# Attention stage of a hybrid encoder layer: query swap placed a tile ahead of use, wider buffer rings, memory weights transposed on TensorE alone

## The chip, the cores and the metric

One core of a Trainium2 chip runs one program. The metric is the device time in microseconds (us) from a run of the whole program; the kernel before has three runs. Its engines are called as the profile calls them: PE (TensorE; PEld its weight loads), DVE (VectorE), ACT (ScalarE), POOL (GpSimd), and SP (SyncE), which here does nothing but issue DMAs. Each engine takes its own instructions strictly in order.

## What is computed

Two sequences (4096 and 1024 tokens, width 1024) go through one layer. A combined projection gives Hyena channels, six attention heads, four memory heads and gates. The part that matters here is the attention:

```python
for window, dil in ((128, 1), (512, 4), (2048, 16)):      # dilated windows
    logits = einsum(q_blocks, k_band) * scale + bias       # masked to |rel| <= R
    p = exp(logits - max); s = sum(p)
    outs.append(einsum(p, v_band) / s); lses.append(m + log(s))
y_att = sum(softmax(lses) * outs)                          # merged over the windows
p = softmax(einsum('blhe,bmhe->bhlm', qm, km) * scale)     # 4 heads, 256 memory tokens
y_mem = einsum('bhlm,bmhe->blhe', p, vm)
out = x + (concat(hyena, y_att, y_mem) * silu(gate)) @ w_out
```

## The kernel before, in words

The program weaves two streams on PE. `dense()` projects queries, keys and values and then, in `gates`, the gates (products into tile `zg`, 1920 matmuls through the helper `mm3`, lines 282 to 284). `side()` does the long convolutions, the memory keys and values, and then `attention`. `weave` gives the next piece to the stream whose sum of nominal costs is lower; the costs are what the generators `yield`, and those of attention are scaled by `K_A` = 0.88 while gates run. PE's order is exactly the order in which this is written. The order on the other engines is chosen when the program is built: a list scheduler places each instruction where its own simulated clock finds it ready, and breaks ties by priority, which is the order of emission.

Attention works on 84 groups of up to 256 query rows: 64 groups of the dilated windows, 8 of which are pairs of 64-row sequences, and 20 memory groups. A group has two tiles of 128 rows (a pair has one), so there are 160 tiles, 120 of windows and 40 of memory.

- `load_group` (lines 923 to 973) loads a group two groups ahead (`AHEAD` = 2): DMA transposes bring `qT` (lines 948, 943, 935 for memory) and `kT` (947, 942), plain DMAs bring `v`. For a window group it ends with two DVE copies that swap the halves of the queries, `qS<-qT` (line 971), in a ring of two buffers. Memory groups have no swap.
- `scores` (lines 1005 to 1058) makes products `s` on PE from `qT` (1048) and `qS` (1051), or from `kmT` for memory (1043). DVE reduces each head at once into `pt` with its row maximum `mx` (line 1055). `s` has three PSUM buffers.
- `exps` (1060 to 1070) negates the maximum on DVE (`nm`, 1065) and takes exponentials on ACT (1067). After two heads (`XT` = 2) it calls `crossbar`, which on POOL splits the two heads into halves `hl` (1083, 1084) and issues one DMA transpose `hx<-hl` (1086) on SP.
- `turns` (1090 to 1105) transposes the other heads on PE, two at a time (`tt`, line 1098, four 128x128 blocks, two PSUM buffers), and ACT and DVE copy them out as `th` and `tl` (1102, 1103), four buffers each.
- `values` (1107 to 1127), four tiles behind the scores (`VLAG`), multiplies `th`, `tl` and `hx` with `v` into `yp`, and `attended` brings it out through `y`, two buffers (POOL line 1156, ACT 1157, or DVE 1150 for memory) and a store on SP.

Within a step the four generators take turns by the string `ORDER = "etevsteeesvvsetesvsetse"` (s scores, e exponentials, t turns, v values). When attention ends, the output stage begins: it loads `w_out` (`wos`), splits it, merges the windows (`y<-yc` to `ya`), and its products `oo` start when the last gate product is done.

Of the kernel before, what the change touches and what calls it, by code (L numbers as in the profile page):

```python
# [12 lines left out]
F32 = mybir.dt.float32  # L13
F32R = mybir.dt.float32r
F16 = mybir.dt.float16
# [7 lines left out]
P = 128  # L23
# [3 lines left out]
H = 6  # L27
# [11 lines left out]
YW = VH + H  # L39
# [108 lines left out]
XT, VLAG = 2, 4  # L148
# [33 lines left out]
class Layer:  # L182
# [745 lines left out]
    def load_group(self, pool, g):  # L928
        i, nc = g["seq"], self.nc
        dil, r = g.get("dil", 1), g.get("r", 0)  # L930
        rows = self.rows[i].rearrange("(n d) c -> d n c", d=dil)
        vr = self.vrows[i].rearrange("(n d) c -> d n c", d=dil)
        qT = g["qT"] = pool.tile([P, 6, 256], F16, tag="qT", name="qT", bufs=AHEAD + 1)
        if "mem" in g:
            nc.sync.dma_start_transpose(out=qT[:, 0:4], in_=self.rows[i][g["q0"]:g["q0"] + 256, C_MQ:C_K])
            return
        kT = pool.tile([P, 6, 384], F16, tag="kT", name="kT", bufs=AHEAD + 1)
        nk = g["k1"] - g["k0"]
        v = pool.tile([P, 3, VW], F16, tag="v", name="v", bufs=2)
        if g["pair"]:  # L940
            for a in range(2):
                nc.sync.dma_start_transpose(out=kT[:, :, 64 * a:64 * a + 64], in_=rows[r + a, :, C_K:ROW])
                nc.sync.dma_start_transpose(out=qT[:, :, 64 * a:64 * a + 64], in_=rows[r + a, :, C_Q:C_MQ])
                self.ld(v[64 * a:64 * a + 64, 0, :], vr[r + a])
            g["chunks"] = {0: 0}
        else:
            nc.sync.dma_start_transpose(out=kT[:, :, :nk], in_=rows[r, g["k0"]:g["k1"], C_K:ROW])
            nc.sync.dma_start_transpose(
                out=qT[:, :, :g["nq"]], in_=rows[r, g["q0"]:g["q0"] + g["nq"], C_Q:C_MQ]
            )  # L950
            cuts = [g["k0"]] + list(range(g["q0"] + 64, g["k1"], 128))
            ends = cuts[1:] + [g["k1"]]
            g["chunks"] = {s: j for j, s in enumerate(cuts)}
            full = [j for j, (s, e) in enumerate(zip(cuts, ends)) if e - s == 128]
            part = [j for j, (s, e) in enumerate(zip(cuts, ends)) if e - s != 128]
            if full:
                f0, nf = full[0], len(full)
                assert full == list(range(f0, f0 + nf))
                self.ld(
                    v[:, f0:f0 + nf, :],  # L960
                    vr[r, cuts[f0]:cuts[f0] + 128 * nf].rearrange("(j p) c -> p j c", p=P),
                )
            for j in part:
                k = ends[j] - cuts[j]
                p0 = P - k if j else 0
                nc.gpsimd.memset(v[P - k:P, j, :] if p0 == 0 else v[0:p0, j, :], 0.0)
                self.ld(v[p0:p0 + k, j, :], vr[r, cuts[j]:ends[j]])
        g["kT"], g["v"] = kT, v
        qS = g["qS"] = pool.tile([P, 6, 256], F16, tag="qS", name="qS", bufs=2)
        for a in range(2):  # L970
            nc.vector.tensor_copy(  # L971
                qS[64 * a:64 * a + 64, :, :g["nq"]], qT[64 - 64 * a:P - 64 * a, :, :g["nq"]]
            )
# [18 lines left out]
    def attention(self, pool, ps):  # L992
        nc = self.nc
        zero = pool.tile([P, 1], F32, name="zero", bufs=1)
        nc.vector.memset(zero, 0.0)
        groups = self.work_list()
# [3 lines left out]
        self.load_tables(pool)  # L1000
        for g in groups[1:AHEAD]:
            self.load_group(pool, g)
        yield IDLE_A
        tiles = [(gi, t) for gi, g in enumerate(groups) for t in range(g["nq"] // P)]
        state = {}

        def scores(n):
            gi, t = tiles[n]
            g = groups[gi]
            if t == 0 and gi + AHEAD < len(groups):  # L1010
                while groups[gi + AHEAD]["seq"] not in self.done:
                    yield 500
                self.load_group(pool, groups[gi + AHEAD])
            mem = "mem" in g
            i, q0 = g["seq"], g["q0"] + t * P
            st = state[n] = dict(g=g, q0=q0, mem=mem, H=HM if mem else H)
            if mem:
                W, ls = NMEM, self.lsc[:, 1, 0:1]
                st["chunks"] = [(0, 0), (P, 1)]
                st["v"], st["lo"] = self.vm[i], HM * E1  # L1020
                units = ((0, 1), (2, 3))
            else:
                ls = self.lsc[:, 0, 0:1]
                if g["pair"]:
                    ks, ke, tb, t0 = 0, 128, self.tabp, 0
                    st["chunks"] = [(0, 0)]
                else:
                    ks, ke = max(0, q0 - 64), min(g["n"], q0 + 192)
                    tb, t0 = self.tab[g["cf"]], ks - (q0 - 64)
                    st["chunks"] = [(0, g["chunks"][ks]), (ke - ks - P, g["chunks"][q0 + 64])]  # L1030
                W, kc = ke - ks, ks - g["k0"]
                st["v"], st["lo"] = g["v"], VH
                units = ((0, 2), (1, 3), (4,), (5,))
            st["W"] = W
            pt = st["pt"] = pool.tile([P, H, 256], F32, tag="pt", name="pt", bufs=3)
            mx = st["mx"] = pool.tile([P, H], F32, tag="mx", name="mx", bufs=4)
            qs = slice(t * P, (t + 1) * P)
            for heads in units:
                s = ps.tile([P, 2, 256], F32, tag="f", name="s", bufs=3)
                for a, h in enumerate(heads):  # L1040
                    if mem:
                        for half in range(2):
                            nc.tensor.matmul(
                                s[:, a, :], g["qT"][:, h, qs], self.kmT[i][:, 4 * half + h, :],
                                start=(half == 0), stop=(half == 1),
                            )
                        continue
                    nc.tensor.matmul(  # L1048
                        s[:, a, :W], g["qT"][:, h, qs], g["kT"][:, h, kc:kc + W], start=True, stop=False,
                    )  # L1050
                    nc.tensor.matmul(  # L1051
                        s[:, a, :W], g["qS"][:, h, qs], g["kT"][:, h, kc:kc + W], start=False, stop=True,
                    )
                for a, h in enumerate(heads):
                    nc.vector.tensor_tensor_reduce(  # L1055
                        out=pt[:, h, :W], in0=s[:, a, :W], in1=zero.to_broadcast([P, NMEM]) if mem else tb[:, h, t0:t0 + W], scale=ls,
                        scalar=-3.0e38, op0=ALU.add, op1=ALU.max, accum_out=mx[:, h:h + 1],
                    )
                yield 215 * len(heads)

        def exps(n):
            st = state[n]
            nh, pt, W = st["H"], st["pt"], st["W"]
            nm = st["nm"] = pool.tile([P, H], F32, tag="nm", name="nm", bufs=VLAG + 1)
            nc.vector.tensor_scalar_mul(nm[:, :nh], st["mx"][:, :nh], -1.0)  # L1065
            for h in range(nh):
                nc.scalar.activation(out=pt[:, h, :W], in_=pt[:, h, :W], func=AF.Exp, bias=nm[:, h:h + 1])  # L1067
                if h + 1 == XT:
                    crossbar(st)
                yield 0  # L1070

# [18 lines left out]
        def turns(n):  # L1090
            st = state[n]
            pt, chunks = st["pt"], st["chunks"]
            st["p"] = []
            for pr in range(XT // 2, st["H"] // 2):
                tt = ps.tile([P, 2, 2, P], F32, tag="e", name="tt", bufs=2)
                for ci, (w0, vj) in enumerate(chunks):
                    for a in range(2):
                        nc.tensor.transpose(tt[:, a, ci, :], pt[:, 2 * pr + a, w0:w0 + P], self.ident)  # L1098
                th = pool.tile([P, 2, 2, P], F16, tag="th", name="th", bufs=4)
                tl = pool.tile([P, 2, 2, P], F16, tag="tl", name="tl", bufs=4)  # L1100
                n = len(chunks)
                nc.scalar.activation(out=th[:, :, :n], in_=tt[:, :, :n], func=AF.Copy)  # L1102
                nc.vector.tensor_tensor(out=tl[:, :, :n], in0=tt[:, :, :n], in1=th[:, :, :n], op=ALU.subtract)  # L1103
# [3 lines left out]
        def values(n):  # L1107
            st = state[n]
            chunks, v, lo = st["chunks"], st["v"], st["lo"]
            last = len(chunks) - 1  # L1110
            yp = ps.tile([P, 512], F32, tag="gf"[n % 2], name="yp", bufs=(1, 3)[n % 2])
            heads = list(range(XT, st["H"])) + list(range(XT))
            st["p"] += [(st["hx"][:, 0, h], st["hx"][:, 1, h]) for h in range(XT)]
            for pr in range(st["H"] // 2):
                for a in range(2):
                    h = heads[2 * pr + a]
# [23 lines left out]
    def attended(self, pool, st, yp):  # L1140

        nc = self.nc
        g, q0 = st["g"], st["q0"]
        y = pool.tile([P, YW], F32, tag="y", name="y", bufs=2)
        if st["mem"]:
            sm = pool.tile([P, HM], F32, tag="sm", name="sm", bufs=3)
            yv = yp[:, :HM * E1].rearrange("p (h e) -> p h e", e=E1)
# [528 lines left out]
```

## Time and profile before

| | |
|---|---|
| median of 3 runs | 3090.1 us (3088.88 to 3095.87) |
| the profiled execution | 3090.2 us, its span 3088.4 us |
| PE busy | 2783.8 us, 90% of the span |
| DVE / ACT / POOL busy | 2087.6 / 1690.0 / 1350.3 us |
| chain that ended last, by engine | PE 27%, DMA 10%, DVE 7% |
| its largest single entry | DMA `qT<-rows`, 6% |

The span runs from the first to the last instruction of the core; the run's own time is 1.8 us longer. PE is busy for most of the span, so the question for a stretch is what it idles for. A wait is named after what ended it. "PEclk" is the mean clock that was granted to PE as a share of full speed; the records know two levels, 1.2 and 2.4 GHz, so 0.5 and 1.0.

### The profile page before, as it was taken

To read this page: it belongs to the slowest core of one execution; us is meant where nothing else is said; L and a number is where in the kernel's file an instruction comes from. 1 tells how busy PE (TensorE), PEld (TensorE's weight loads), DVE (VectorE), ACT (ScalarE), POOL (GpSimd) and SP (SyncE) were. 2 spreads that over 40 slices of the span, in tenths; PEclk is the share of its full clock that TensorE was granted. 3 is DMA by queue.
4 is the path that set the end of the run, shared out by engine and by line. 5 is a ranking of instruction groups with operands and counts; after the bars stand their busy time and mean duration, and the time that the engine had idled before them with its cause. 6 is when DMAs were issued, how large, how long until landed. Compare 5 with 4: busy or idle time off the path is not lost. (4 is left out here: it accounts for less than half of the span.)

```text
span 3088.4 us, 55692 instructions
## 1 busy us (share of the span) xinstructions
PE 2783.8 (90%) x19620; PEld 1724.7 (56%) x19620; DVE 2087.6 (68%) x5374; ACT 1690.0 (55%) x3187; POOL 1350.3 (44%) x1574
## 2 busy tenths in 40 slices
PE   5898888988999887986998989999898899999999
PEld 2343444434544444543456666676666665778887
DVE  8778888778757861452657766776666666766663
ACT  5776666433679873472336666666565564323321
POOL 3246777343236661252324333343243443655551
PEclk9999999999999999998999999999999999999999
DMA  7655444565588867585679999999898989777762
GB/s 195 199 154 161 134 127 136 172 180 185 197 233 226 217 179 200 219 178 114 178 183 250 225 208 212 224 227 189 200 220 194 196 176 305 259 235 252 247 227 97
DMA packets 761954, 610.80 MB, mean 198 GB/s; under 512 B 514814, under 2 KB 702358, under 8 KB 758218
## 3 DMA queue, kind: packets, MB, share of 16 engines
q1 hardware_dynamic: 761674, 607.23, 73.7%
q8 instruction: 155, 2.54, 0.3%
q14 instruction: 125, 1.02, 0.1%
HBM read 289.08 MB, written 200.32 MB: 158 GB/s over the span
## 5 line engine op out<-in xcount | busy, mean ns | idle before, releaser
L1067 ACT ACTIVATE pt<-pt,nm 128x256 f32<-128x256 f32 (+2 forms) x880 | 349.8, 472 | 175.9 <-DVE nm L1065 170.0
L282 PE MATMUL z<-wA,hA 128*128 128x512 f16 (+1 forms) x960 | 352.7, 367 | 34.9 <-DVE vr L476 23.6
L283 PE MATMUL z<-wA,hA 128*128 128x512 f16 (+1 forms) x960 | 352.6, 367 | 0.0
L284 PE MATMUL z<-wA,hA 128*128 128x512 f16 (+1 forms) x960 | 352.3, 367 | 0.0
L1055 DVE CUSTOM_DVE_ANT_0 pt<-s,tab,lsc 128x256 f32<-128x256 f32 (+1 forms) x672 | 277.7, 448 | 83.2 <-PE s L1051 73.5
L282 PE MATMUL zh<-hB,wh 128*128 128x512 f16 x720 | 279.8, 389 | 15.1 <-ACT zb L879 14.8
L283 PE MATMUL zh<-hB,wh 128*128 128x512 f16 x720 | 279.5, 388 | 1.6 <-DVE hB L387 1.6
L284 PE MATMUL zh<-hB,wh 128*128 128x512 f16 x720 | 278.9, 387 | 0.0
L282 PE MATMUL oo<-wo,mhi 128*128 128x512 f32 x640 | 257.2, 402 | 8.2 <-DVE xr L1553 2.5
L284 PE MATMUL oo<-wo,mlo 128*128 128x512 f32 x640 | 253.9, 397 | 0.4 <-POOL mlo L1532 0.4
L283 PE MATMUL oo<-wo,mhi 128*128 128x512 f32 x640 | 253.7, 396 | 0.0
L282 PE MATMUL zg<-hG,wg 128*128 128x512 f16 x640 | 246.8, 386 | 0.0
L283 PE MATMUL zg<-hG,wg 128*128 128x512 f16 x640 | 246.5, 385 | 0.0
L284 PE MATMUL zg<-hG,wg 128*128 128x512 f16 x640 | 246.1, 385 | 0.0
L1083 POOL CAST hl<-pt 128x256 f16<-128x256 f32 (+1 forms) x212 | 104.1, 505 | 320.0 <-ACT pt L1067 242.9
L1103 DVE TENSOR_TENSOR tl<-tt,th 128x512 f16<-128x512 f32 (+1 forms) x280 | 187.5, 672 | 58.5 <-ACT th L1102 56.9
L1102 ACT ACTIVATE th<-tt 128x512 f16<-128x512 f32 (+1 forms) x280 | 160.1, 574 | 117.6 <-PE yp L1124 54.3
L1048 PE MATMUL s<-kT,qT 128*128 128x256 f16 (+2 forms) x720 | 165.1, 260 | 45.0 <-DVE mx L1055 43.3
L1098 PE MATMUL tt<-ident,pt 128*128 128x128 f32 x1088 | 171.9, 280 | 30.0 <-DVE tl L1103 25.4
L1338 ACT ACTIVATE kt<-kp,rn 64x384 f32<-64x384 f32 x328 | 188.0, 573 | 13.6 <-PE kp L1332 8.4
L1084 POOL TENSOR_TENSOR hl<-pt,hl 128x256 f16<-128x256 f32 (+1 forms) x212 | 191.4, 910 | 6.8
L893 DVE SCALAR_TENSOR_TENSOR u<-zb,cw,u 128x512 f32<-128x512 f32 (+2 forms) x180 | 163.4, 910 | 25.0 <-ACT u L889 23.2
(303 smaller groups left out, 7277.9 us busy)
## 6 DMA issues: line engine op xcount, KB each, us to landing
y<-yc SPq DMA_DIRECT2D x120, 198.0 KB
yc<-y SPq DMA_DIRECT2D x112, 198.0 KB
xt<-in_x SPq DMA_DIRECT2D x40, 512.0 KB
hts<-hB SPq DMA_DIRECT2D x10, 2048.0 KB
hA<-hts SPq DMA_DIRECT2D x40, 512.0 KB
rows<-rw SPq DMA_DIRECT2D x40, 512.0 KB
hG<-hts SPq DMA_DIRECT2D x10, 2048.0 KB
gt<-go SPq DMA_DIRECT2D x80, 256.0 KB
```

Source lines behind the costliest of these rows:

```text
L282: nc.tensor.matmul(out, pick_l(lh, k), pick_r(rh, k), start=(k == 0), stop=False)
L283: nc.tensor.matmul(out, pick_l(lh, k), pick_r(rl, k), start=False, stop=False)
L284: nc.tensor.matmul(out, pick_l(ll, k), pick_r(rh, k), start=False, stop=(k == n - 1))
L893: nc.vector.scalar_tensor_tensor(out=u[:, :w], in0=zb[:, c0 + d:c1 + d], scalar=cw[:, j, tap:tap + 1], in1=u[:, :w], op0=ALU.mult, op1=ALU ...
L1048: nc.tensor.matmul(s[:, a, :W], g["qT"][:, h, qs], g["kT"][:, h, kc:kc + W], start=True, stop=False,)
L1055: nc.vector.tensor_tensor_reduce(out=pt[:, h, :W], in0=s[:, a, :W], in1=zero.to_broadcast([P, NMEM]) if mem else tb[:, h, t0:t0 + W], scal ...
L1067: nc.scalar.activation(out=pt[:, h, :W], in_=pt[:, h, :W], func=AF.Exp, bias=nm[:, h:h + 1])
L1084: nc.gpsimd.tensor_tensor(out=hl[:, 1, :, c], in0=src, in1=hl[:, 0, :, c], op=ALU.subtract)
L1098: nc.tensor.transpose(tt[:, a, ci, :], pt[:, 2 * pr + a, w0:w0 + P], self.ident)
L1102: nc.scalar.activation(out=th[:, :, :n], in_=tt[:, :, :n], func=AF.Copy)
L1103: nc.vector.tensor_tensor(out=tl[:, :, :n], in0=tt[:, :, :n], in1=th[:, :, :n], op=ALU.subtract)
L1338: nc.scalar.activation(out=kt[64 * b:64 * b + 64, a], in_=kp[64 * a:64 * a + 64, :DH], func=AF.Identity, scale=rn[64 * a:64 * a + 64, a * ...
```

## The change

The swap leaves `load_group` and becomes a function of its own. It is called for the first group before the loop, and for every later group at the start of the last tile of the group ahead of it. Memory tiles get `xt` = 0 in place of `XT` = 2: no `crossbar`, no `hl` and `hx`, and a second turn on PE for the two heads that went through them. `th` and `tl` have six buffers in place of four, `y` four in place of two.

```diff
         g["kT"], g["v"] = kT, v
+
+    def swap_queries(self, pool, g):
+
+        if "mem" in g:
+            return
+        nc, qT = self.nc, g["qT"]
         qS = g["qS"] = pool.tile([P, 6, 256], F16, tag="qS", name="qS", bufs=2)
         for a in range(2):
             nc.vector.tensor_copy(
...
         for g in groups[1:AHEAD]:
             self.load_group(pool, g)
+        self.swap_queries(pool, groups[0])
         yield IDLE_A
...
                 self.load_group(pool, groups[gi + AHEAD])
+            if (t + 1) * P == g["nq"] and gi + 1 < len(groups):
+                self.swap_queries(pool, groups[gi + 1])
             mem = "mem" in g
...
                 W, ls = NMEM, self.lsc[:, 1, 0:1]
-                st["chunks"] = [(0, 0), (P, 1)]
+                st["chunks"], st["xt"] = [(0, 0), (P, 1)], 0
...
+                st["xt"] = XT
                 W, kc = ke - ks, ks - g["k0"]
...
-                if h + 1 == XT:
+                if h + 1 == st["xt"]:
                     crossbar(st)
...
-            for pr in range(XT // 2, st["H"] // 2):
+            for pr in range(st["xt"] // 2, st["H"] // 2):
...
-                th = pool.tile([P, 2, 2, P], F16, tag="th", name="th", bufs=4)
-                tl = pool.tile([P, 2, 2, P], F16, tag="tl", name="tl", bufs=4)
+                th = pool.tile([P, 2, 2, P], F16, tag="th", name="th", bufs=6)
+                tl = pool.tile([P, 2, 2, P], F16, tag="tl", name="tl", bufs=6)
...
-            heads = list(range(XT, st["H"])) + list(range(XT))
-            st["p"] += [(st["hx"][:, 0, h], st["hx"][:, 1, h]) for h in range(XT)]
+            heads = list(range(st["xt"], st["H"])) + list(range(st["xt"]))
+            st["p"] += [(st["hx"][:, 0, h], st["hx"][:, 1, h]) for h in range(st["xt"])]
...
-        y = pool.tile([P, YW], F32, tag="y", name="y", bufs=2)
+        y = pool.tile([P, YW], F32, tag="y", name="y", bufs=4)
```

The built programs show where the instructions went. First DVE at the swap of one window group in the middle of attention; the rows are in DVE's order, numbers tell buffers apart, and lines of the changed kernel are 10 further down (977 is the swap, 1065 the reduction, 1075 `nm`, 1113 `tl`). Before:

```order
L1055 ISA pt_17844,mx_17845<-s_17897,tab0_15041,lsc_849 128x256
L1055 ISA mx_17845 128x1
L971 COPY qS_17744<-qT_17738 64x1536 x2
L1055 ISA pt_17844,mx_17845<-s_17902,tab0_15041,lsc_849 128x256
L1055 ISA mx_17845 128x1
L1103 TENSOR_TENSOR tl_17915<-tt_17909,th_17914 128x512
L1065 TENSOR_SCALAR nm_17906<-mx_17845 128x6
```

The same group in the changed program:

```order
L1065 ISA pt_17865,mx_17866<-s_17932,tab0_15038,lsc_849 128x256
L1065 ISA mx_17866 128x1
L1065 ISA pt_17865,mx_17866<-s_17940,tab0_15038,lsc_849 128x256
L1065 ISA mx_17866 128x1
L977 COPY qS_18082<-qT_17747 64x1536 x2
L1075 TENSOR_SCALAR nm_17944<-mx_17866 128x6
L1113 TENSOR_TENSOR tl_17953<-tt_17947,th_17952 128x512
```

`pt_17844` and `pt_17865` are the same tile, the last of the group two ahead of the swapped one. The swap went from ahead of that tile's sixth reduction to behind it; it was emitted a whole group later, as its number 18082 tells, and did not move by a group.

Second, SP between one query load and the next that are followed by the two tiles of a memory group. Before:

```order
L948 DMA_TRANSPOSE qT_21138<-rows0_75 128x6x256
L195 DMA v_20694<-vrows1_106 128x774
L195 DMA v_20694<-vrows1_106 64x774 x2
L1086 DMA_TRANSPOSE hx_21021<-hl_21018 128x8x128
L198 DMA yc0_0_83<-y_21097 128x396
L1086 DMA_TRANSPOSE hx_21120<-hl_21117 128x8x128
L198 DMA yc0_1_84<-y_21192 128x396
L195 DMA v_20929<-vrows0_76 128x3x774
L198 DMA gt0_2_89<-go_21305 128x512
L198 DMA yc0_1_84<-y_21292 128x396
L1086 DMA_TRANSPOSE hx_21228<-hl_21223 128x8x128
```

In the changed program:

```order
L948 DMA_TRANSPOSE qT_21198<-rows0_75 128x6x256
L198 DMA gt0_2_89<-go_21162 128x512
L195 DMA v_20767<-vrows1_106 128x774
L195 DMA v_20767<-vrows1_106 64x774 x2
L198 DMA yc0_0_83<-y_21158 128x396
L198 DMA yc0_1_84<-y_21261 128x396
L195 DMA hG_15482<-hts0_4_99 128x8192
L195 DMA v_20999<-vrows0_76 128x3x774
L198 DMA gt0_2_89<-go_21381 128x512
L1096 DMA_TRANSPOSE hx_21294<-hl_21289 128x8x128
```

The two DMA transposes of the memory tiles (`hx_21021`, `hx_21120`) are gone; a 2 MB load of the gates (`hG`) has come forward into the stretch.

## Rows read from the trace of the kernel before

**Rows 1.** Busy time by stretch: stretch, us, PE, PEld, DVE, ACT, POOL, PEclk, DMA share, GB/s

```profile
1588.00:2562.00 974.00, 888.01 (x9878) 633.60 (x9876) 673.92 (x2479) 597.34 (x1370) 364.11 (x606) 0.97 0.97 211
2562.00:2603.50 41.50, 40.63 (x191) 18.60 (x189) 22.69 (x43) 18.72 (x23) 12.84 (x9) 1.00 0.98 351
2603.50:3088.40 484.90, 472.93 (x2115) 381.17 (x2115) 299.98 (x666) 140.51 (x173) 250.74 (x191) 1.00 0.66 224
```

**Rows 2.** Waits of PE, 1588 to 2562 us: total us, times, longest

```profile
PE s L1048 <- DVE mx L1055: 43.3, 32, 5.6
PE tt L1098 <- DVE tl L1103: 25.4, 22, 3.0
PE s L1043 <- DVE mx L1055: 5.9, 3, 4.4
```

**Rows 3.** DVE in order of time, around one swap: start, us, what, idle before

```profile
2178.90 0.42 DVE L1103 TENSOR_TENSOR tl<-tt,th 128x256 f16<-128x256 f32 x1
2184.45 1.12 DVE L971 COPY qS<-qT 64x1536 f16<-64x1536 f16 x2 [5.13 <-DMA qT<-rows]
```

**Rows 4.** PE in order of time, the same moment

```profile
2181.34 0.38 PE L284 MATMUL zg<-hG,wg 128*128 128x512 f16 x1
2186.15 1.01 PE L1043 MATMUL s<-kmT,qT 128*128 128x256 f16 x4 [4.43 <-DVE mx L1055]
...
2187.81 0.63 PE L282 MATMUL zg<-hG,wg 128*128 128x512 f16 x1
```

**Rows 5.** Waits of the other engines, 1588 to 2562 us

```profile
POOL hl L1083 <- ACT pt L1067: 242.9, 98, 7.2
...
POOL y L1156 <- DMA yc<-y: 158.2, 63, 6.2
DVE qS L971 <- DMA qT<-rows: 105.9, 44, 6.2
...
ACT th L1102 <- PE yp L1124: 54.3, 50, 3.8
```

**Rows 6.** SP's issues in order of time, ahead of that swap's query load

```profile
2163.67 3.48 SPq L935 DMA_TRANSPOSE qT<-rows  x1
2167.25 4.64 SPq L1086 DMA_TRANSPOSE hx<-hl  x1
2171.99 0.53 SPq L198 DMA_DIRECT2D ym<-y  x1
2172.61 2.12 SPq L947 DMA_TRANSPOSE kT<-rows  x1
...
2180.53 1.46 SPq L948 DMA_TRANSPOSE qT<-rows  x1
```

**Rows 7.** Instructions on tile hx: SP's issues, ns min/median/max

```profile
L1086 SPq DMA_TRANSPOSE hx<-hl x160: 1206/1271/5327, 1608.2 to 2556.8; - x160
```

**Rows 8.** DMA packets, 1588 to 2562 us

```profile
DMA packets 453444, 205.96 MB, mean 211 GB/s; under 512 B 400590, under 2 KB 441792, under 8 KB 451904
```

**Rows 9.** Chain that ended last, two turns: start, us, what

```profile
1906.67 0.44 PE tt L1098 x4
...
1924.62 0.85 PE tt L1098 x4
```

**Rows 10.** Groups of instructions by form, 1588 to 2562 us: busy us, mean ns

```profile
L1103 DVE TENSOR_TENSOR tl<-tt,th 128x512 f16<-128x512 f32 x264 | 180.9, 687 | 56.7 <-ACT th L1102 55.1
...
L1102 ACT ACTIVATE th<-tt 128x512 f16<-128x512 f32 x264 | 154.1, 586 | 107.6 <-PE tt L1098 45.2 <-PE yp L1124 44.8 <-PE yp L1123 17.1
```

**Rows 11.** ACT in order of time, the last tile of attention

```profile
2561.46 0.50 ACT L1157 ACTIVATE y<-yp 128x390 f32<-128x390 f32 x1 [1.37 <-PE yp L1124]
```

**Rows 12.** DVE in order of time, the first merged tile of the output

```profile
2593.39 0.55 DVE L1504 TENSOR_TENSOR ya<-y 128x384 f32<-128x384 f32 x1
```

**Rows 13.** PE in order of time, the first output product

```profile
2603.53 0.50 PE L282 MATMUL oo<-wo,mhi 128*128 128x512 f32 x1 [0.90 <-ACT mhi L1531]
```

## The prediction

> **What bounds the kernel now.** I read the busy time by stretch first. Attention, woven with gate products, takes the stretch from 1588 to 2562 us [rows 1]: PE is busy for 888 of 974 us there, so 86 us are idle; the change touches nothing before it. The stretch's DMA share is 0.97 and no other engine is busy for more than 70%. The waits of PE say what the idle time is for: 43.3 + 25.4 + 5.9 = 74.6 us until DVE has freed a PSUM buffer, of scores or of a turn [rows 2]. So DVE is late, though it is idle for 300 us. The two timelines show why. DVE ends its work at 2179.3, reaches a swap whose query load has not landed, and stands for 5.13 us [rows 3]; PE runs on until its buffers are full and then stands for 4.43 us [rows 4]. All in all DVE stands 105.9 us, 44 times, in front of a swap [rows 5], 1.65 us for each of the 64 swaps. And the load is late because SP comes late to it: its issues follow each other within 0.1 us, transposes of 3.48, 4.64 and 2.12 us among them, until the load goes out at 2180.5 [rows 6], after DVE had begun to wait. So the chain is SP and the DMA engines, then DVE at the swap, then PE.
>
> **The change, part by part.** The sum is made against the profiled execution's 3090.2 us, 0.1 us above the median of the three runs.
>
> *The swap itself* costs the same copies, 64 pairs in both programs. Its words promise a load two tiles more to land. The built order does not keep that promise: in both programs the swap stands behind the scores of the group two ahead, where its buffer comes free, because the scheduler is at liberty to bring an instruction forward. Over the 64 swaps I count in the order 13.2 reductions (a little over two tiles) between a swap and the first one that needs it before, 13.0 now. The query loads stand where they were on SP too: 8.1 tiles ahead of use by the stores that precede them, in both. So I price this edit at nothing. What it does move is the sixth reduction of the tile, now mostly ahead of the swap, which frees one more score buffer before a wait, and `nm`, now mostly behind it, which holds ACT. I let them cancel.
>
> *Memory tiles.* Forty tiles lose `hx` and gain a turn. On PE a turn of four transposes takes 0.44 us at full clock and 0.85 us at half [rows 9]: 17.6 to 34 us, and with a mean clock of 0.97, that is 6% of the time at half clock, 19 us. All of this is added to PE's queue and none of it is hidden. ACT gets 40 x 0.586 = 23 us and DVE 40 x 0.687 = 27 us [rows 10]; they are covered by the 377 and 300 us that these engines idle in the stretch, and if DVE's cover failed the 27 us would come on top. POOL loses the splitting, worth nothing, since it is busy for 364 us only.
>
> *What the missing `hx` gives back.* SP spends 1.271 us on an issue [rows 7] and rarely pauses, so 40 issues are 51 us of its time, or 0.80 us for each of the 64 intervals between swaps, against a wait of 1.65 us: 48%. The DMA engines gain too. Their 0.97 of 974 us is 945 us for 206 MB. Packets under 512 B are 400590 [rows 8], and a row of a transposed block is 256 B by the code, so 103 MB are transposes and 103 MB plain. The plain stretch behind moves 351 GB/s at a share of 0.98 [rows 1], so the plain bytes take 289 us and the transposes 656 us, 1.6 ns a packet. One `hx` is eight blocks of 128 rows; 40 of them are 40960 packets, 67 us of 945. The Trainium skill (Advanced Engine Details and Errata, X-Bar Transpose) says otherwise: "TRN2 transpose DMAs are as fast as regular DMAs". By that the `hx` would give back less than half of the 67 us, and the sum would near the second rival's; the trace speaks against it, with 211 GB/s at 0.97 beside 351 GB/s at 0.98. Between all of PE's 74.6 us kept and all of it gone I take the 48%: 36 us.
>
> *The clock.* After the wait at 2186 the same gate product stands for 0.63 us in place of 0.38 [rows 4], so PE was then granted the lower of its two levels. With 6% of 974 us at half clock about 29 us of work are lost in the stretch, at most all of it is won back, at least nothing; I take a third, 10 us.
>
> *The buffers.* POOL stands 158.2 us for the store of `y`, and ACT 54.3 us for the values that free `th` [rows 5]; both waits should go. Neither engine holds PE directly. POOL's lateness delays `hx` and thereby SP, but 98 times `hl` waits for ACT and not for POOL [rows 5]. Bounds: nothing, or the 39 us of stalls that the term above leaves. I take 6 us, near the lower end, because the work behind these waits is mostly early. Next in line is ACT's exponential for `nm`.
>
> *The end of attention.* A turn counts 430 in the weave, so attention's stream advances more slowly against gates and takes more of them with it: in PE's order 120 gate products stand behind attention's last value product, 189 before. The 69 are only moved. But they covered something: attention ends at 2562.0 [rows 11], the first merged tile that the output needs is ready at 2593.9 [rows 12], 32.0 us later, and the gates behind lasted until then, so that the first output product waits 0.90 us only [rows 13]. Now they last 120 x 40.63/191 = 25.5 us, and PE stands 6 us. At best loads start earlier and this is nothing; at worst the next tiles come late too, 15 us.
>
> Sum: 3090.2 + 19 - 36 - 10 - 6 + 6 = 3063 us.
>
> **The rivals.** *Nothing is given back.* The loads' place in SP's order, not SP's load, makes them late: SP then waits for PE and POOL instead of for itself, DVE still stands 106 us. Then PE pays for the turns and the join: 3090 + 19 + 6 = 3115 us. For it: the order is the same, and at the end of a stretch SP also waits for buffers. Against it: the closed row of issues in rows 6. It decides if less than a third of the 74.6 us goes.
>
> *Only bytes count.* SP's gaps are then filled by waiting for the DMA engines, and a transposed byte takes no longer than a plain one: 40 x 0.262 MB at 351 GB/s [rows 1] are 30 of 945 us, 3%. Stalls and clock then give back a tenth, 10 us: 3105 us. The Trainium skill (DMA: Bandwidth & Descriptors, Issuing engines are not separate DMA queues) has such a rule: initiating a DMA takes sequencer time that is "usually small relative to the DMA itself". Here an issue holds SP 1.271 us [rows 7], and SP issues back to back [rows 6], which speaks against the rival.
>
> *It cancels.* Stalls and clock give back about 25 us, a third less than I take, and the turns and the join eat it: 3090 us.
>
> *All stalls go.* The backlog on SP is a matter of bursts, and a tenth less load ends it, or the loads do come earlier as the change says: 3090 + 25 - 75 - 29 = 3011 us. Against it speaks that loads of 2 MB for the gates remain, one of which now stands ahead in the row that the order shows.
>
> **How the numbers follow.** My forecast has 0.56, all stalls gone 0.14, cancelled 0.13, nothing given back 0.09, bytes alone 0.08. A measurement of this kernel tells about 0.2%, 6 us, from no change. Faster is the forecast and the third gain, 0.70; the same 0.13; slower 0.17. The range reaches from the fast rival to just short of the slow two, 3010 to 3098 us, which leaves 0.17 out; it covers the bounds of the turns (17.6 to 34), of the join (0 to 15) and of the stalls (a quarter of them to all).
>
> **What would show it.** In the changed profile the wait of DVE for `qT` should be 45 to 70 us, not near zero and not 106; PE's waits for DVE some 40 us; the waits of `y` on POOL and of `th` on values nearly gone; 1248 transposes of `tt`, not 1088; PE idle for some 7 us before the first output product; attention some 25 us shorter. If DVE still stands for 100 us at the swap the explanation by SP's load is wrong; if it stands for none, the swap or the load moved after all.

## The result and the profile after

The changed kernel took 3111.5 us (median of 4 runs, 3107.4 to 3116.6), the kernel before 3089.5 us. The ratio of the two is 1.0064, with a 95% interval from 1.0042 to 1.0087: **slower by 20 us**, where I had forecast 27 us faster. The profiled execution of the changed kernel has a span of 3105.6 us, 17.2 us more than that of before.

I cut both traces at three events on PE: the first score product, attention's last value product, the first output product. In brackets stands the time in which PE idled.

| us (PE idle) | before | changed |
|---|---|---|
| up to the first score product | 1592.6 | 1591.4 |
| to attention's last value product | 968.7 (86.0) | 981.9 (71.0) |
| to the first output product | 42.2 (0.9) | 34.1 (7.3) |
| to PE's end | 480.6 (7.7) | 493.9 (18.2) |

69 gate products more lie ahead of the last value product in the changed kernel; at 40.63/191 us each [rows 1] they are 14.7 us. Without them attention took 967.2 us, 1.5 us less than before. I had forecast 33 us less (19 - 36 - 10 - 6). Behind attention 8.1 of those 14.7 us came back, so 6.6 us were lost, and the output then took 13.3 us longer. So all of the loss lies behind attention, and the gain that should have outweighed it did not come.

The same stretch as in rows 1, then the first 40 us of the output (stretch, us, PE, PEld, DVE, ACT, POOL, PEclk, DMA share, GB/s):

```profile
1588.00:2562.00 974.00, 903.43 (x9927) 648.66 (x9926) 678.80 (x2500) 615.62 (x1398) 288.04 (x518) 0.97 0.89 199
...
2600.00:2640.00 40.00, 24.12 (x97) 19.26 (x98) 31.10 (x62) 13.46 (x17) 26.40 (x20) 0.79 0.94 319
```

The DMA engines have 8% of the stretch to themselves that they had not before (share 0.89 for 0.97), and yet PE's granted clock stands at 0.97 as it did. The waits, 1588 to 2600 us, which answer to rows 2 and 5:

```profile
POOL hl L1093 <- ACT pt L1077: 330.4, 77, 16.2
DVE qS L977 <- DMA qT<-rows: 110.8, 43, 5.8
POOL y L1166 <- DMA yc<-y: 81.8, 35, 7.5
PE s L1058 <- DVE mx L1065: 48.5, 32, 5.0
PE tt L1108 <- DVE tl L1113: 15.5, 11, 4.3
```

DVE waits for its query loads 110.8 us, not 45 to 70; before it was 105.9. PE's waits for DVE add to 64 us, not 40. The wait of `y` was halved and that of `th` on values is gone. SP's issues ahead of a late query load, in order of time, show why fewer issues did not help:

```profile
2141.88 0.54 SPq L198 DMA_DIRECT2D yc<-y  x1
2145.44 1.48 SPq L195 DMA_DIRECT2D v<-vrows  x3
2147.14 0.42 SPq L198 DMA_DIRECT2D gt<-go  x1
2147.66 2.50 SPq L1096 DMA_TRANSPOSE hx<-hl  x1
2150.21 0.58 SPq L198 DMA_DIRECT2D yc<-y  x1
2150.88 1.45 SPq L948 DMA_TRANSPOSE qT<-rows  x1
```

SP ended an issue at 2142.4, issued nothing for 3 us until 2145.44, and then took 2.50 us for an `hx`, about twice the median of rows 7. So SP had time to spare, and the query load behind still went out at 2150.88 only. DVE's swap was ready for it 3.35 us before it could start:

```profile
2155.01 1.12 DVE L977 COPY qS<-qT 64x1536 f16<-64x1536 f16 x2 [3.35 <-DMA qT<-rows]
```

Over 1588 to 2565 us I summed SP's DMA issues, each split into the shortest tenth's time of its kind and what lies above it, and the gaps between them: the shortest times fell from 554.5 to 497.9 us, while gaps and excess rose from 415.1 to 472.4 us. All of the rise is in the gaps, from 178.2 to 248.1 us; the excess inside the issues went from 236.9 to 224.3 us. **What SP no longer issued became gaps between its issues.**

The start of the output, on ACT (attention's last tile), DVE (the first merged tile) and PE:

```profile
2573.31 0.50 ACT L1167 ACTIVATE y<-yp 128x390 f32<-128x390 f32 x1 [0.40 <-PE yp L1134]
```

```profile
2605.85 0.52 DVE L1514 TENSOR_TENSOR ya<-y 128x384 f32<-128x384 f32 x1
```

```profile
2598.79 0.38 PE L284 MATMUL zg<-hG,wg 128*128 128x512 f16 x1
2606.42 1.33 PE L1535 MATMUL ot<-ident,ya 128*128 128x128 f32 x5 [7.25 <-DVE ya L1514]
2607.40 0.78 PE L282 MATMUL oo<-wo,mhi 128*128 128x512 f32 x1
...
2630.11 1.30 PE L1535 MATMUL ot<-ident,ya 128*128 128x128 f32 x5 [9.33 <-DVE mw L1504]
```

The first merged tile is ready 33 us after attention's end, as before [rows 11, 12], but the gates end 7 us earlier than that. PE waits 7.25 us, which I had forecast as 6. I had not forecast the second wait, 9.33 us, 24 us later. The first output product behind the first wait takes 0.78 us and not 0.50 [rows 13], and the granted clock of these 40 us is 0.79.

### The profile page after: what moved, and what is told of

Read it like the earlier page. It is cut to its first block, busy times and chain, and to the rows that moved or that the text cites. A ratio compares the mean times of both kernels' runs of the same rounds, so it can differ in the third digit from the quotient of the medians.

```text
span 3105.6 us, 55808 instructions
## 1 busy us (share of the span) xinstructions
PE 2802.1 (90%) x19780; PEld 1746.0 (56%) x19780; DVE 2094.8 (67%) x5414; ACT 1713.0 (55%) x3227; POOL 1275.3 (41%) x1494
## 5 line engine op out<-in xcount | busy, mean ns | idle before, releaser
L282 PE MATMUL zh<-hB,wh 128*128 128x512 f16 x720 | 279.8, 389 | 15.0 <-ACT zb L879 14.7
L1113 DVE TENSOR_TENSOR tl<-tt,th 128x512 f16<-128x512 f32 (+1 forms) x320 | 214.3, 673 | 64.5 <-ACT th L1112 63.0
L1093 POOL CAST hl<-pt 128x256 f16<-128x256 f32 (+1 forms) x172 | 78.8, 476 | 433.2 <-ACT pt L1077 330.4
L1112 ACT ACTIVATE th<-tt 128x512 f16<-128x512 f32 (+1 forms) x320 | 182.2, 574 | 125.2 <-PE tt L1108 124.2
L1108 PE MATMUL tt<-ident,pt 128*128 128x128 f32 x1248 | 194.8, 278 | 19.2 <-DVE tl L1113 15.5
L1348 ACT ACTIVATE kt<-kp,rn 64x384 f32<-64x384 f32 x328 | 188.0, 573 | 13.2 <-PE kp L1342 8.1
L1108 PEld LDWEIGHTS tt<-ident,pt 128*128 128x128 f32 x1248 | 150.6, 143 | 55.4 <-issue 14.9
```

Source lines behind the costliest of these rows:

```text
L282: nc.tensor.matmul(out, pick_l(lh, k), pick_r(rh, k), start=(k == 0), stop=False)
L1093: nc.gpsimd.tensor_copy(hl[:, 0, :, c], src)
L1348: nc.scalar.activation(out=kt[64 * b:64 * b + 64, a], in_=kp[64 * a:64 * a + 64, :DH], func=AF.Identity, scale=rn[64 * a:64 * a + 64, a * ...
```

## The experiments

Two theories stood after the result. **SP's time** (the prediction): the issues themselves make the query loads late. **The place**: the load stands where the order puts it on SP, and whatever is taken off SP ahead of it only becomes a wait. For the loss there was one more question: is the join worth 6 us or much more? Each ratio is to runs of the kernel before on the same chip, 95% interval in brackets; DVE's wait is that for `qT` between 1588 and 2600 us, PE's idle time that of attention in the profiled execution; "gates behind" are the gate products behind attention's last value product.

| run | edit | ratio | DVE's wait | PE idle | gates behind |
|---|---|---|---|---|---|
| (before) | | 1 | 105.9 | 86.0 | 189 |
| (changed) | | 1.0064 [1.0042, 1.0087] | 110.8 | 71.0 | 120 |
| x1 | before, 40 `hx` left out | 0.9946 [0.9921, 0.9970] | 103.6 | 85.5 | 189 |
| x2 | before, swap moved | 1.0005 [0.9987, 1.0022] | 109.5 | 88.7 | 189 |
| x3 | before, memory on TensorE | 1.0082 [1.0056, 1.0107] | 95.8 | 72.8 | 120 |
| x4 | before, buffers | 0.9958 [0.9941, 0.9975] | 117.7 | 81.0 | 189 |
| y1 | changed, weave mended | 0.9985 [0.9970, 1.0001] | 100.1 | 70.7 | 189 |
| y2 | before, weave spoilt | 1.0084 [1.0062, 1.0106] | 108.7 | 90.3 | 120 |
| y3 | x4, swap cut | 0.9919 [0.9900, 0.9937] | 65.4 | 66.9 | 189 |
| y4 | changed, swap cut | 0.9925 [0.9902, 0.9948] | 53.2 | 42.7 | 120 |
| z1 | y1, swap cut | 0.9904 [0.9880, 0.9928] | 51.0 | 55.8 | 189 |
| z2 | y1, queries ahead | 0.9836 [0.9812, 0.9860] | 46.9 | 41.3 | 189 |
| z3 | z1, queries ahead | 0.9807 [0.9779, 0.9834] | 10.2 | 33.0 | 189 |
| z4 | y1, stores on ACT | 0.9979 [0.9962, 0.9996] | 107.0 | 65.4 | 189 |
| w1 | z3, `hx` back | 0.9841 [0.9819, 0.9863] | 7.2 | 56.7 | 189 |
| w2 | z3 again | 0.9795 [0.9773, 0.9817] | 9.6 | 34.1 | 189 |

### The change in parts

**x1**, SP's relief without its price:

```diff
+            if st["mem"]:
+                return
             hx = st["hx"] = pool.tile([P, 2, XT, n, P], F16, tag="hx", name="hx", bufs=3)
...
-            st["p"] += [(st["hx"][:, 0, h], st["hx"][:, 1, h]) for h in range(XT)]
+            st["p"] += st["p"][:XT] if st["mem"] else [(st["hx"][:, 0, h], st["hx"][:, 1, h]) for h in range(XT)]
```

> The kernel before with the 40 DMA transposes of hx of the memory tiles left out and nothing put in their place: the value products of these tiles' first two heads read the transposed weights of the other two heads, so PE, ACT, POOL and DVE have the work of before. This leaves out the transposing of two heads in 40 tiles, whose part of the output is then not attention. If SP's issue time makes the query loads late (the prediction): 36 us of stalls and some 10 us of clock come back without a price, 3044 us, and DVE's wait for qT falls from 106 to about 55 us. If the load's place in SP's order makes it late (SP then waits for the producers of the stores and transposes ahead of the load): within 6 us of 3090 us, DVE's wait for qT stays at 95 to 115 us, and SP's waits grow by about the 50 us that the issues took. If transposed bytes on the DMA engines make it late: 3040 to 3060 us too, with shorter landings.

Measured: 17 us faster (9 to 24), neither 46 nor nothing. Its stretch and its waits, 1588 to 2562 and to 2600 us:

```profile
1588.00:2562.00 974.00, 888.53 (x9912) 633.42 (x9911) 681.20 (x2480) 599.50 (x1372) 364.05 (x606) 0.98 0.90 202
```

```profile
DVE qS L971 <- DMA qT<-rows: 103.6, 39, 6.0
...
PE s L1048 <- DVE mx L1055: 37.6, 25, 3.9
PE tt L1100 <- DVE tl L1105: 19.9, 17, 2.6
```

DVE's wait stays, PE idles as long as before (85.5 us), SP's shortest times fall by 54 us and its gaps rise by 61 (from 178.2 to 239.4 us), while the excess inside its issues stays (236.9 and 235.5 us). SP's time as the cause of the wait has fallen. Where the 17 us are from is not settled: attention was 6.9 us shorter in this execution at the same idle time, with the granted clock at 0.98 for 0.97.

**x2**, the swap alone, is the new method with its two calls:

```diff
         g["kT"], g["v"] = kT, v
+
+    def swap_queries(self, pool, g):
...
+            if (t + 1) * P == g["nq"] and gi + 1 < len(groups):
+                self.swap_queries(pool, groups[gi + 1])
```

> The kernel before with the first edit alone: the swap is emitted one tile ahead of use. Prediction: the built order leaves it two tiles ahead, so nothing, 3084 to 3096 us, DVE's wait for qT about 105 us. Rival: the sixth reduction, which now mostly stands ahead of the swap, frees one more score buffer before the wait, and that is where the 15 us of stalls went that the changed kernel has less in attention: 3075 us, PE's waits for DVE 60 us in place of 75.

Measured: 1.5 us slower (4 faster to 7 slower), DVE's wait 109.5 us. An edit whose words promise something, and which the built order does not carry out, did nothing.

**x3**, the memory tiles alone, with the buffers and the swap of before:

```diff
-                st["chunks"] = [(0, 0), (P, 1)]
+                st["chunks"], st["xt"] = [(0, 0), (P, 1)], 0
...
-            for pr in range(XT // 2, st["H"] // 2):
+            for pr in range(st["xt"] // 2, st["H"] // 2):
```

> The kernel before with the third edit alone: memory tiles transposed on TensorE, buffers and swap as before. Prediction: 3090 + 19 (turns) - 36 - 10 + 6 = 3069 us. If the place in SP's order decides, nothing comes back: 3090 + 19 for the turns + 16 for two stalls at the start of the output (as in the changed kernel) = 3125 us, or 3110 us if the 15 us less of stalls in attention belong to this edit. DVE's wait for qT 50 to 60 us by the first, 100 to 115 us by the second.

Measured: 25 us slower (17 to 33). This part holds the whole loss.

**x4**, the buffers alone, is `tl` as shown, `th` likewise, and `y`:

```diff
-                tl = pool.tile([P, 2, 2, P], F16, tag="tl", name="tl", bufs=4)
+                tl = pool.tile([P, 2, 2, P], F16, tag="tl", name="tl", bufs=6)
...
-        y = pool.tile([P, YW], F32, tag="y", name="y", bufs=2)
+        y = pool.tile([P, YW], F32, tag="y", name="y", bufs=4)
```

> The kernel before with the second edit alone: 6 buffers for th and tl, 4 for y. Prediction: 6 us faster, 3084 us, with the wait of y on POOL (158 us) and of th on values (54 us) nearly gone. If POOL and ACT are off the path: no change, 3090 us, with the waits gone all the same. If the 15 us less of stalls in the changed kernel's attention belong to this edit: 3075 us.

Measured: 13 us faster (8 to 18). The wait of `th` on values is gone and that of `y` is smaller, not gone:

```profile
POOL y L1156 <- DMA yc<-y: 94.4, 36, 5.0
```

The buffers were worth twice what I took. By which way they reach PE is not shown; PE's idle time in attention is 5 us less (81.0 for 86.0).

### The join

**y1** takes the weight of the memory tiles' second turn out of the weave, **y2** puts it into the kernel before. No work is added or left out; the weave places gate products elsewhere, 69 of them from attention to behind it (y1) or the other way (y2).

```diff
-                yield 430
+                yield 430 if st["xt"] else 215
```

```diff
-                yield 430
+                yield 860 if st["mem"] else 430
```

> The changed kernel with one number changed: a turn of a memory tile counts 215 in the weave in place of 430, so the two turns count what one did, and 189 gate products stand behind attention's last value product again, not 120. Nothing else is computed otherwise. If the preparation of the output is bound from attention's end on, for two merged blocks (my theory after the first runs): the two waits at the start of the output (7.3 and 9.3 us) go, and the half clock behind them, some 17 us: 1.001 of the time before. By the prediction, which priced this at 6 us: 1.0045. If the gates in attention filled stalls there that now stay open: no change, 1.006.

> The kernel before with the same number turned the other way: the one turn of a memory tile counts 860 in place of 430, so that 120 gate products stand behind attention's last value product, not 189. The work is the same on every engine. If the join is worth all of the 69 gates and the half clock behind the waits: 15 to 20 us slower, 1.005 to 1.006, with two waits of 6 to 10 us at the start of the output. By the prediction: 6 us, 1.002, with one wait.

Measured: y1 is 4.6 us faster than before, not clear of noise (9.3 us faster to 0.3 slower), and 24 us better than the changed kernel; y2 is 26 us slower (19 to 33). **A number of the weave, without any work added, costs as much as the whole loss of the change.** The waits of PE in y2, 2560 to 2680 us, are those of the changed kernel:

```profile
PE ot L1525 <- DVE mw L1494: 9.3, 1, 9.3
PE ot L1525 <- DVE ya L1504: 7.3, 1, 7.3
```

and the start of the output in y2 and in y1, 40 us from 7.4 us ahead of the first output product, as in the stretch of the changed kernel above:

```profile
2618.80:2658.80 40.00, 22.65 (x88) 17.91 (x89) 28.00 (x59) 12.81 (x16) 23.67 (x19) 0.74 0.90 306
```

```profile
2588.00:2628.00 40.00, 37.18 (x169) 27.07 (x167) 32.02 (x66) 15.00 (x19) 26.56 (x23) 1.00 0.85 275
```

In y2 the way from attention's end to the output is 34.7 us, 7.2 more than 42.2 - 14.7, and the output takes 500.7 us for 480.6, with 14.9 us more of PE idle in it. The first merged tile is ready 32.6 to 33.7 us behind attention's last value product in all four kernels (before, changed, y1, y2), the third 51 us behind it in before and y1, 57 to 60 us in the others. So the gates behind attention cover the preparation of the first tile and also what comes after it, and a gate that is moved ahead is not merely moved. Why the third tile comes later was not followed up.

### The swap and its load

**The swap cut into tiles** (y3, y4, z1): a `qS` for each tile, so that a swap can stand only one tile ahead of use. In the built order it now stands 8.3 score reductions ahead, where it was 13.

```diff
-        qS = g["qS"] = pool.tile([P, 6, 256], F16, tag="qS", name="qS", bufs=2)
+        qS = g["qS", t] = pool.tile([P, 6, P], F16, tag="qS", name="qS", bufs=2)
...
-            if (t + 1) * P == g["nq"] and gi + 1 < len(groups):
-                self.swap_queries(pool, groups[gi + 1])
+            if "mem" not in g:
+                self.swap_queries(pool, g, t)
```

> The kernel before with the buffers of the change (th and tl 6, y 4) and a swap that is cut into tiles: each tile has a qS of its own of 128 queries, in two buffers, so that its swap cannot stand more than one tile ahead of use, where the group's could stand two. The memory tiles keep hx. If the swap that waits on DVE for its load is what holds PE (the chain of the prediction): a load has one tile, 6 us, more before DVE comes to it, against a mean wait of 2.4 us; DVE's wait for qT falls from 106 to under 30 us, PE's waits for DVE from 75 to about 25 us, 50 us with some clock on top of the 13 us of the buffers: 0.98 of the time before. If PE has to wait for the late swap itself, or for other work that is late by then: 0.992 to 0.996, what the buffers alone give, with waits of PE for qS in place of those for mx.

> The changed kernel with the same swap cut into tiles, in two buffers; memory tiles on TensorE, 120 gates behind attention. If the swap's wait holds PE: 50 us less than the changed kernel, 0.99 of the time before, DVE's wait for qT under 30 us. If not: 1.006, as the changed kernel.

> The changed kernel with both edits of the second runs: the swap cut into tiles in two buffers, and a turn of a memory tile that counts 215, so that 189 gates stand behind attention. If the two add up: the changed kernel with the swap cut (0.9925) less what the join gave in the changed kernel (1.0064 - 0.9985 = 0.0079): 0.985 of the time before, 3045 us beside 3090, with PE idle for some 45 us in attention and for 8 us in the output. If the memory tiles on TensorE bring nothing once the join is mended: 0.992, as the kernel before with buffers and the cut swap.

Measured: 12 us better than x4 (y3), 43 us better than the changed kernel (y4), 25 us better than y1 (z1). Each time DVE's wait falls by 50 us or so and PE's idle time by 14 to 28, and no wait of PE for `qS` comes up. That chain of the prediction holds: DVE at the swap, then PE. But only in part: for y3 I had set 50 us, and its 0.9919 lies next to the other guess (0.992 to 0.996), so there the waits decide and not the time. The wait does not vanish, and the gains don't add up: y4 and y1 together would have been 0.985, z1 is at 0.9904. Why z1 idles 13 us more than y4 was not followed up.

**z2** leaves the swap's call as the change has it and emits the queries' loads a group earlier, into one buffer more (`y` has three buffers for that, y1 four); **z3** does both, with `y` at four.

```diff
-        qT = g["qT"] = pool.tile([P, 6, 256], F16, tag="qT", name="qT", bufs=AHEAD + 1)
+        qT = g["qT"] = pool.tile([P, 6, 256], F16, tag="qT", name="qT", bufs=AHEAD + 2)
...
+                far = groups[min(gi + AHEAD + 1, len(groups) - 1)]
...
                 self.load_group(pool, groups[gi + AHEAD])
+                if gi + AHEAD + 1 < len(groups):
+                    self.load_queries(pool, far)
```

> The changed kernel with the join mended (0.9985) and the group's swap as the change has it, but the queries' loads emitted three groups ahead and not two, in four qT buffers (y has three buffers, so that it fits): in SP's order they stand 1.8 tiles, some 11 us, earlier. The issues of SP are the same in number. If the load's place in SP's order is what makes DVE wait at the swap, and that wait is what holds PE: DVE's wait for qT falls from 100 to under 30 us, 0.985. If SP or the DMA engines have no time for it anyway: the wait stays over 80 us, 0.998.

> The last two together: queries' loads three groups ahead, swap cut into tiles, join mended. If the wait for the load is what both take away: hardly better than either, 0.983, DVE's wait for qT under 15 us, and what is left of PE's idle time in attention waits for reductions and turns as such. If cutting the swap works by the shorter copies: the two gains add up, 0.975.

Measured: z2 takes 0.9836 of the time before, 46 us less than y1, with as many issues on SP; z3 takes 0.9807, nearer to the guess that both take away the same wait (0.983) than to the sum of the two gains (0.975). Waits in z2, then in z3, 1588 to 2600 us:

```profile
DVE qS L986 <- DMA qT<-rows: 46.9, 14, 8.3
PE s L1073 <- DVE mx L1080: 14.2, 9, 5.0
```

```profile
PE yp L1144 <- DMA v<-vrows: 15.0, 6, 4.0
PE s L1070 <- DVE mx L1077: 13.3, 12, 4.8
DVE qS L984 <- DMA qT<-rows: 10.2, 3, 7.7
```

The load's place decides, then: the same loads, 1.8 tiles earlier in SP's order, take away half of the wait (46.9 for 100.1 us) that 40 fewer issues had left standing. A later swap is not the reason: by the order in the traces it stands 15.6 reductions ahead of its first use in z2, 12.6 in y1. Whether the earlier emission or the fourth buffer is what lets the loads go ahead was not separated. In z3 PE's longest wait in attention is no longer for DVE but for the loads of `v`, which I had not named.

**z4** takes the stores of whole window tiles off SP.

```diff
-            self.st(dst[g["r"], q0:q0 + P], y)
+            nc.scalar.dma_start(out=dst[g["r"], q0:q0 + P], in_=y)
```

> The changed kernel with the join mended (0.9985) and the stores of whole window tiles issued from ACT's queue in place of SP's, some 110 of them. If the loads are late because they stand on SP behind stores that wait for their y: DVE's wait for qT falls from 100 to 50 to 70 us, 0.990 to 0.994. If the buffers that PE frees hold the loads: the wait stays at 90 to 110 us, 0.998 to 1.002, and ACT has some 40 us more to do.

Measured: 0.9979, as y1, with DVE's wait at 107.0 us. My narrower guess, that the loads stand behind stores that wait for their `y`, is wrong; here too SP has less to issue and DVE waits as long. Both numbers are those of the other guess, that buffers which PE frees hold the loads. But that is not shown either: in the kernel before, SP pauses for more than 0.2 us directly ahead of a query load only 14 times, 18 us in all. Which of the entries ahead of a late load holds it stays open.

### What the memory tiles are worth by themselves

> The fastest version (queries loaded three groups ahead, swap cut into tiles, buffers, 189 gates behind attention) with the memory tiles back on the DMA transpose hx. If TensorE's turns cost PE their 19 us and the DMA transposes they replace cost nothing once the loads are early: 19 us less than 0.9807, 0.975 of the time before. If the 40 hx still cost some 17 us (what leaving them out gave in the kernel before): no difference, 0.981. If SP or POOL falls behind with them: 0.985 or more, with DVE's wait for qT back at over 30 us.

> The fastest version again, on the same chip as the last: 0.981 of the time before, for the comparison with it.

w1 is z3 with these two lines, on one chip with w2, which is z3 again:

```diff
-                st["chunks"], st["xt"] = [(0, 0), (P, 1)], 0
+                st["chunks"], st["xt"] = [(0, 0), (P, 1)], XT
...
-                yield 430 if st["xt"] else 215
+                yield 430
```

Measured: 0.9841 against 0.9795, two intervals that just do not overlap, so **TensorE's turns are 14 us better than the 40 `hx`**, once loads come early and the join is mended. The stretch from 1590 to 2510 us in w1 and w2:

```profile
1590.00:2510.00 920.00, 863.70 (x9710) 619.53 (x9709) 700.37 (x2567) 590.63 (x1350) 356.97 (x597) 0.99 1.02 224
```

```profile
1590.00:2510.00 920.00, 885.91 (x10059) 645.32 (x10058) 711.51 (x2629) 620.25 (x1411) 290.80 (x527) 0.99 0.96 214
```

A wait of POOL in w1, 1588 to 2600 us, then the waits of PE for transfers in attention, of w1 and of w2:

```profile
POOL hl L1105 <- DMA hx<-hl: 198.5, 48, 11.6
```

```profile
PE yp L1144 <- DMA v<-vrows: 16.6, 6, 8.6
PE yp L1144 <- DMA hx<-hl: 12.4, 6, 4.0
```

```profile
PE yp L1144 <- DMA v<-vrows: 15.3, 6, 4.1
...
PE yp L1144 <- DMA hx<-hl: 0.2, 1, 0.2
```

With `hx` back the DMA share is 1.02 (w2: 0.96), POOL stands 198.5 us for transposes (w2: 51.0) and PE itself for their results. POOL's wait was there before the loads were early, but shorter: 61.0 us in the kernel before, 104.6 in y3. PE's wait for `hx` was 3.2 us in y3 and none in the kernel before.

## Why the prediction was wrong, by its steps

- **What bounds the kernel.** That DVE at the swap holds PE was right (y3, y4, z2). The next link, "the load is late because SP comes late to it", was read from a row of issues without gaps [rows 6]. From that one row I took that SP "rarely pauses". Over 1588 to 2565 us of the same trace SP has 99 gaps of more than 0.2 us, 125 us in all; in x1 they come to 192 us, and DVE waits as long as before, as it does in the changed kernel (110.8 us). The longest issue in the row (an `hx` of 4.64 us where the median is 1.271 [rows 7]) did not wait for its input: taken in order, the `hl` of each of the 160 `hx` was complete before its issue began. What makes issues long is not shown; with 40 fewer of them the excess stayed as it was.
- **What the missing `hx` gives back**, -36, and **the clock**, -10: x1 gave 17 us in place of 46, with DVE's wait at 103.6. This is the first step that failed, by 29 us. The 48% came from dividing SP's freed time by DVE's wait, and x1 shows that the one does not pass into the other: PE's idle time in attention stayed (85.5 for 86.0 us), so the 36 us of stalls did not come back. The DMA term itself was well sized: the share in the stretch fell from 0.97 [rows 1] to 0.90 in x1, some 68 us of engine time, where I had 67. The Trainium skill (Advanced Engine Details and Errata, X-Bar Transpose) has transposes as fast as plain transfers; by that, as an estimate from the 351 GB/s of rows 1, some 30 us would have gone, so the trace does not agree. But 68 us freed on the DMA engines did not shorten DVE's wait either.
- **The end of attention**, +6: the wait I named came (7.25 us), and behind it a second one (9.33 us) and the lower clock; the join is worth 26 us in y2 and 24 between the changed kernel and y1, most of it behind attention (7.2 and 20.1 us in y2's trace). This is the second step that failed, by about 20 us. My bound ("at worst the next tiles come late too, 15 us") named what happened and was still too small.
- **Memory tiles**, +19: no run has this term by itself. PE's busy time rose from 2783.8 to 2802.1 us, 18.3 us, but in y2 it rose to 2798.0 us without a product added. From w1 to w2, at the same mean clock of 0.98, it rose by 13.2 us. So 19 is of the right size, and not shown more closely.
- **The buffers**, -6: 13 us in x4. **The swap itself**, nothing: 1.5 us in x2, within what can be told. The order showed that rightly.
- **The sum** with the measured terms and the 19 as forecast: 19 - 17 - 13 + 1.5 + 26 = 16.5 us slower; measured 20 (13 to 27). For x3: 19 - 17 + 26 = 28; measured 25.
- **The rivals.** "Nothing is given back" (3115 us) came nearest and had the right mechanism for the loads; I gave it 0.09. That its number came within 4 us is luck: it has nothing for the buffers (-13) and for x1's 17 us, and 6 us for a join that is worth 26. What I held against it was rows 6, some 17 us of SP; the gaps of the whole stretch speak for it. My own test, DVE at 100 us at the swap, decided as I had said it would.

## What to carry to other kernels

A few microseconds without gaps do not show that a queue is short of time: sum its gaps over the whole stage before taking load off it, and if there are many, move the late transfer ahead instead, with a buffer for it. Work that is "only moved" from behind a stage into it may have been covering the next stage's preparation; look at the second and third tile there too, not only at the first wait. And a change can hide a good part: the memory tiles on TensorE are worth 14 us in the fastest version, where a weight in the weave and the place of the loads had been put right (0.9795 of the time before, 63 us). With the join alone mended they brought nothing that can be told: y1 is at 0.9985, the buffers alone (x4) at 0.9958.

## What the runs showed of the hardware

Forty transposes fewer took 54 us from the sum of SP's shortest issue times and gave 61 us to the gaps between its issues (x1). On the DMA engines those 40, some 10.5 MB, had taken 68 us. With the queries loaded early the DMA engines reach a share of 1.02 at 224 GB/s in attention (w1), over the 0.97 at 211 GB/s of before [rows 1], so a share of 0.97 had not been their end. With PE's waits of 7.3 and 9.3 us at the join the granted clock of the 40 us around them is 0.79 (changed kernel) and 0.74 (y2), where y1, without the waits, has 1.00.
